# Moving one of four sums of squares from ScalarE to VectorE at the start of a hybrid encoder block

## The chip, the cores and the metric

The kernel runs on one NeuronCore of one Trainium2 chip. The metric is the time of one execution on the device in microseconds (us). Before the change the median of three runs is 943.38 us, the lowest 943.36 and the highest 943.39.

A core has five engines that run at the same time, each through its own list of instructions and strictly in the order of that list: TensorE (PE in the profile, with its weight loads as PEld), VectorE (DVE), ScalarE (ACT), GpSimd (POOL) and SyncE (SP), which here only issues transfers. An instruction that needs another engine's result waits for a semaphore, and everything behind it on its own engine waits with it.

## The reference

One layer is computed for 256 prompt tokens and 2048 sample tokens, each with 16 learned meta tokens in front. What matters here is its beginning: each token's row of 1024 numbers is divided by the root of the mean of its squares and weighted, and one large projection follows.

```python
def rmsnorm(x, w):
    xf = x.astype(jnp.float32)
    y = xf * lax.rsqrt(jnp.mean(xf * xf, axis=-1, keepdims=True) + NORM_EPS)
    return (y * w.astype(jnp.float32)).astype(x.dtype)

def hybrid_layer(z, norm_w, w_in, ...):
    h = rmsnorm(z, norm_w)
    proj = jnp.einsum('bld,de->ble', h, w_in)
    q, k, v, g_att, c_val, c_glu, g_conv = jnp.split(proj, SPLIT_IDX, axis=-1)
    ...  # windowed attention, gated convolution with layer norm, output projection
    return z + jnp.einsum('ble,ed->bld', mixed, w_out)
```

## The kernel before

The 2320 rows (16 meta tokens, then 18 blocks of 128 tokens) are worked in six groups of columns: the first has 400 (the meta tokens and blocks 1 to 3), the others 384. For each group the normalised rows are wanted transposed, split in a high and a low part (`xh`, `xl`), and then multiplied with eleven units of the input weights (`ws`, split in the same way; lines 863 and 879, tile `pj`). This projection, the attention and the output projection keep TensorE at work to the end.

The first group is made differently from the others, since nothing is there yet to hide it. For its four pieces `i` = 0 (16 meta rows) and 1 to 3 (128 rows each), which are called xn0 to xn3 here:

1. `stats(i)` issues the load of the rows (line 719) and returns a function `rest`. Called later, `rest` squares the rows on ScalarE and sums them along the row (`ssq`, line 726: an `ACTIVATE` and a short `ACTIVATION_READ_ACCUMULATOR`), and calls `rsqrt`, which is two GpSimd instructions: line 148 scales the sum and adds epsilon, line 149 raises it to the power of -1/2 and writes column `i` of `rstd`.
2. VectorE multiplies the rows with `rstd` (line 1131).
3. TensorE multiplies the identity a few times to stay busy (line 1096, `warmup`; 10, 5, 2 and 3 times, each in the trace two matmuls) and transposes the first six of the eight column blocks of 128 (line 1103, tile `xt`).
4. When all four pieces are transposed, ScalarE makes `xh` (line 1111) and VectorE `xl` (line 1113), block by block, between the same split of the first weights (lines 838 and 839), and TensorE starts on `pj`.

Pieces 4 to 6 (the second group) are squared later on ScalarE, at about 19 us; their `rstd` columns go through TensorE (line 755, tile `bc`) into the scaling of `xt` on VectorE (line 772).

The order on each engine is set by the tile framework's scheduler from its own estimate of the times, except for instructions that are "pinned" to program order (`pinned`, `keep_in_program_order`). The squares, the multiplications of line 1131 and the splits are pinned. The two instructions of `rsqrt` and most loads are not: where they stand on GpSimd and SyncE is the scheduler's decision at build time, and the chip keeps to it.

Tiles come from pools with a fixed number of buffers. `sp`'s tag `xn` has two; the loads of xn5 and xn6 took them in the kernel before.

Of the kernel before, what the change touches and what calls it, by code (L numbers as in the profile page):

```python
# [11 lines left out]
F32 = mybir.dt.float32  # L12
F32R = mybir.dt.float32r
BF16 = mybir.dt.bfloat16
AF = mybir.ActivationFunctionType
ALU = mybir.AluOpType
AX = mybir.AxisListType

P = 128
D = 1024  # L20
# [79 lines left out]
def hymba_kernel(  # L100
# [11 lines left out]
    nc = tc.nc  # L112
# [33 lines left out]
    def rsqrt(dst, src, scale, eps):  # L146
        n = src.shape[-1]
        nc.gpsimd.tensor_scalar(src, src, scale, eps, op0=ALU.mult, op1=ALU.add)  # L148
        nc.gpsimd.tensor_tensor(dst, src, half[: src.shape[0], 0:n], op=ALU.pow)
# [56 lines left out]
    sp = right_pools.enter_context(tc.tile_pool(name="sp", bufs=2, side="right"))  # L206
# [494 lines left out]
    if True:  # L701
# [3 lines left out]
        def pinned(op, yes=True):  # L705
            if yes:
                tc.keep_in_program_order(op)

        def stats(i):
            rows = NM if i == 0 else P  # L710
            r0 = 0 if i == 0 else NM + P * (i - 1)
            if i < 4:
                xn = cp.tile([P, UWID], F32, tag="us", name=f"xn{i}")[:, :D]
                rows0[i] = xn
            elif i == 4:
                xn = yp.tile([P, YW], F32, tag="y", name=f"xn{i}")[:, :D]
            else:
                xn = sp.tile([P, D], F32, tag="xn", name=f"xn{i}")
            dma = nc.sync.dma_start(xn[:rows], z[r0 : r0 + rows, :])
            if i >= PIN_X:  # L720
                tc.keep_in_program_order(dma)

            def rest():
                ssq = sp.tile([P, 1], F32, tag="ssq", name=f"ssq{i}", bufs=4)
                sq = sq0[:, :D] if i < 4 else xn
                pinned(nc.scalar.activation(sq[:rows], xn[:rows], AF.Square, accum_out=ssq[:rows]), i < 10)  # L726
                rsqrt(rstd[:rows, i : i + 1], ssq[:rows], 1.0 / D, EPS)

            return rest
# [363 lines left out]
        def busy(pt, n):  # L1093

            for _ in range(n):
                tc.keep_in_program_order(nc.tensor.matmul(pt[:, :P], ident, ident, start=True, stop=True))

        def turn0(i, d):

            o, rows = SEGS0[i]  # L1100
            if d not in cols0:
                cols0[d] = psum.tile([P, 512], F32, tag="cdcdabcd"[d], name=f"xt0_{d}")
            return nc.tensor.transpose(
                cols0[d][:, o : o + rows], rows0[i][:rows, P * d : P * d + P], ident[:rows, :rows]
            )
# [14 lines left out]
        r = {0: stats(0)}  # L1120
# [5 lines left out]
        nc.sync.dma_start(cw, conv_w)  # L1126
        warmup = psum.tile([P, 512], F32, tag="a", name="warmup")
        for i in range(4):
            r[i]()
            o, rows = SEGS0[i]  # L1130
            pinned(nc.vector.tensor_scalar(rows0[i][:rows], rows0[i][:rows], rstd[:rows, i : i + 1], None, op0=ALU.mult))
            busy(warmup, (10, 5, 2, 3)[i])
            for d in range(6):
                tc.keep_in_program_order(turn0(i, d))
        preps[0].alloc()
        r = {i: stats(i) for i in (4, 5, 6)}
# [56 lines left out]
        for i, (c, u, g) in enumerate(items):  # L1193
# [34 lines left out]
            if c == 0 and u in U_GA:  # L1228
                for k3 in range(3):
                    k = 10 + 3 * (3 * (u - U_GA[0]) + g) + k3  # L1230
# [84 lines left out]
```

## Time and profile before

| | us |
|---|---|
| median of the runs | 943.38 |
| the profiled execution | 943.95 |
| span of its instructions | 941.9 |
| TensorE busy in the span | 935.6 |
| VectorE busy | 744.4 |
| ScalarE busy | 421.8 |
| GpSimd busy | 293.3 |

The profiled execution took 0.57 us more than the median of the runs; 2.05 us of it lie outside the span of its instructions. The profile gives for every instruction the start in us from the span's beginning, the duration, the engine, the line of the kernel and the operation with its tiles; an idle time in front of an instruction stands behind it in brackets, with what ended it.

### The profile page before, as it was taken

The numbers are of one execution on the slowest core, as the hardware profiler recorded it, in microseconds if no ns is written. First come the engines' busy times: TensorE is split into PE (matmuls) and PEld (weight loads), VectorE is DVE, ScalarE is ACT, GpSimd is POOL, SyncE is SP. The second block draws the span as 40 slices with busy tenths as digits, with TensorE's granted clock in tenths as the row PEclk, the third lists the DMA queues.
The fourth block names the chain that finished last, engine by engine and source line by source line (L and its number), as shares of the span: only waits on it lengthen the run. The fifth ranks groups of instructions, "written<-read, shape, count | busy, mean of one in ns | idle before, by whom it ended". The sixth has DMA issues, their size and how long they took to land.

```text
span 941.9 us, 16665 instructions
## 1 busy us (share of the span) xinstructions
PE 935.6 (99%) x5794; PEld 886.3 (94%) x5794; DVE 744.4 (79%) x1263; ACT 421.8 (45%) x1160; POOL 293.3 (31%) x490
## 2 busy tenths in 40 slices
PE   9999999999999999999999999999999999999998
PEld 8999999999999999999999999988888888888887
DVE  5579999997977879999996655677777677767773
ACT  7432022253457751011111356666666666656661
POOL 4320000173558400000000553755433242333332
PEclk9999999999999999999999999999999999999999
DMA  8575345676656595233333697975666556655512
GB/s 306 170 253 217 134 176 176 217 269 251 182 185 189 182 312 182 90 113 134 140 128 123 159 327 225 395 240 159 200 188 172 151 165 196 188 159 148 163 62 68
DMA packets 146211, 176.49 MB, mean 187 GB/s; under 512 B 40816, under 2 KB 108736, under 8 KB 146000
## 3 DMA queue, kind: packets, MB, share of 16 engines
q1 hardware_dynamic: 146128, 175.43, 57.8%
q8 instruction: 46, 0.75, 0.3%
q14 instruction: 37, 0.30, 0.1%
HBM read 112.69 MB, written 62.70 MB: 186 GB/s over the span
## 4 chain that ended last, share of the span: by engine, by line
PE 94%; DMA 2%; DVE 1%; SPq 1%; issue 0%; ACT 0%; POOL 0%; DVEq 0%; ACTq 0%; POOLq 0%
PE pj L863 43%; PE y L609 21%; PE pj L879 13%; PE O L533 5%; PE S L383 4%; PE pT_c L499 2%; PE pT_m L499 2%; PE pT_x L499 1%; DMA cd<-zn 1%; DMA bias<-in_bias_c 1%; PE qT L383 1%; PE lnu L240 0%; DMA xn<-in_z 0%; PE lnt L221 0%; DVE xt L772 0%
## 5 line engine op out<-in xcount | busy, mean ns | idle before, releaser
L863 PE MATMUL pj<-xh,ws 128*128 128x384 f32 (+1 forms) x1536 | 395.9, 338 | 0.1
L946 DVE SCALAR_TENSOR_TENSOR y<-us,cw,y 128x1167 f32<-128x1167 f32 x240 | 329.0, 1427 | 0.4
L863 PEld LDWEIGHTS pj<-xh,ws 128*128 128x128 f32 x1536 | 280.0, 188 | 0.4 <-ACT xh L1111 0.4
L863 PE MATMUL pj<-xl,ws 128*128 128x384 f32 (+1 forms) x768 | 260.9, 340 | 0.1
L609 PE MATMUL y<-wo,rest 128*128 128x512 f32 (+1 forms) x672 | 172.7, 394 | 0.0
L879 PE MATMUL pj<-ws,xh 128*128 128x256 f32 (+1 forms) x880 | 164.2, 284 | 0.3 <-DVE kn L1037 0.3
L863 PEld LDWEIGHTS pj<-xl,ws 128*128 128x128 f32 x768 | 144.1, 188 | 0.5 <-DVE xl L801 0.4
L609 PEld LDWEIGHTS y<-wo,rest 128*128 128x128 f32 x672 | 117.5, 189 | 21.4 <-DVE rest L566 0.3
L879 PEld LDWEIGHTS pj<-ws,xh 128*128 128x128 f32 (+1 forms) x880 | 136.1, 187 | 1.1 <-issue 0.4
L879 PE MATMUL pj<-ws,xl 128*128 128x256 f32 (+1 forms) x440 | 124.3, 283 | 0.0
L441 DVE CUSTOM_DVE_ANT_0 sb<-S,bias,vec 128x304 f32<-128x304 f32 (+5 forms) x144 | 74.5, 517 | 33.8 <-PE S L383 31.5
L453 ACT ACTIVATE sb<-sb,nm 128x304 f32<-128x304 f32 (+5 forms) x144 | 77.8, 540 | 48.9 <-DVE nm L441 48.2
L971 ACT ACTIVATE go<-pj 128x384 f32<-128x384 f32 x48 | 23.5, 489 | 149.8 <-PE pj L863 142.3
L879 PEld LDWEIGHTS pj<-ws,xl 128*128 128x128 f32 (+1 forms) x440 | 82.2, 187 | 0.2
L479 POOL TENSOR_SCALAR sb<-sb,es 128x304 f32<-128x304 f32 (+5 forms) x144 | 73.1, 525 | 16.0 <-DVE es L466 13.1
L561 POOL TENSOR_TENSOR at<-at,ga 128x256 f32<-128x256 f32 x36 | 26.5, 737 | 164.0 <-DVE at L555 104.8
L148 POOL TENSOR_SCALAR ssk<-ssk 128x2 f32<-128x2 f32 x18 | 8.4, 465 | 210.0 <-ACT sqk L985 210.0
L383 PEld LDWEIGHTS S<-kw,q 128*128 128x128 f32 x288 | 53.2, 188 | 10.6
L383 PE MATMUL S<-kw,q 128*128 128x304 f32 (+5 forms) x288 | 62.8, 299 | 0.0
L148 POOL TENSOR_SCALAR ssq<-ssq 128x4 f32<-128x4 f32 (+2 forms) x55 | 23.5, 427 | 98.3 <-ACT xn L726 74.4
L906 ACT ACTIVATE sg<-pj 128x384 f32<-128x384 f32 (+1 forms) x24 | 11.8, 492 | 82.9 <-PE pj L863 82.0
L609 PE MATMUL y<-wo,mch 128*128 128x512 f32 x144 | 47.2, 409 | 0.0
(139 smaller groups left out, 1306.9 us busy)
## 6 DMA issues: line engine op xcount, KB each, us to landing
wd<-ws SPq DMA_DIRECT2D x36, 512.0 KB, 5.8
ws<-wd SPq DMA_DIRECT2D x36, 512.0 KB, 6.2
wraw<-in_w_in SPq DMA_DIRECT2D x52, 256.0 KB, 6.3
xn<-in_z SPq DMA_DIRECT2D x18, 512.0 KB, 5.5
gd<-go SPq DMA_DIRECT2D x48, 192.0 KB, 2.2
yo<-in_z SPq DMA_DIRECT2D x36, 256.0 KB, 3.9
out_y<-yo SPq DMA_DIRECT2D x35, 256.0 KB, 2.7
wo<-wod SPq DMA_DIRECT2D x16, 512.0 KB, 7.4
```

The lines of the kernel that those rows point to most:

```text
L148: nc.gpsimd.tensor_scalar(src, src, scale, eps, op0=ALU.mult, op1=ALU.add)
L383: r = f(*a, **k)
L441: nc.vector.tensor_tensor_reduce(out=sb[:, n, c0:c1], in0=ps[:, 0:w], in1=cst["bias"][:, kv, at + c0 : at + c1], scale=1.0, scalar=nsnk[:, ...
L453: nc.scalar.activation(sb[:, n, c0:c1], sb[:, n, c0:c1], AF.Exp, bias=nm[:, n : n + 1], scale=-1.0, accum_out=rs[:, n : n + 1],)
L479: nc.gpsimd.tensor_scalar(sb[:, k, a0:a1], sb[:, k, a0:a1], es[:, k : k + 1], 1.0, op0=ALU.mult, op1=ALU.mult)
L499: nc.tensor.transpose(pt[: c1 - c0, n, :], sbt[b, kv][:, n, c0:c1], ident)
L533: nc.tensor.matmul(opj[b, kv][:, n0:n1], t[:r, kv, :], p[:r, n0:n1], start=(k == "c" and i == 0), stop=(k == "x" and i == len(work) - 1),)
L561: nc.gpsimd.tensor_tensor(at[:, pr, :], at[:, pr, :], gat[b][:, pr, :], op=ALU.mult)
L609: nc.tensor.matmul(ps, mh[mi][:, e % 4, :], wo[e, wi][:, cols], start=(e == 4 and k == 0), stop=(e == 3 and k == 2),)
L863: nc.tensor.matmul(ps[:, :n], ws[:, d, wi, P * half_i : P * half_i + P], x[xi][:, d, o : o + n], start=(k == 0), stop=(k == 3 * ND - 1),)
L879: nc.tensor.matmul(ps[:rows, :UW], x[xi][:, d, o : o + rows], ws[:, d, wi, :], start=(k == 0), stop=(k == 3 * ND - 1),)
L946: nc.vector.scalar_tensor_tensor(y[:, yo + o0 : yo + o1], u[:, o0 + k : o1 + k], cw[:, j, k : k + 1], y[:, yo + o0 : yo + o1], op0=ALU.mul ...
```

## The change

For piece 2 the squares and their sum are made by one VectorE instruction pair instead (`tensor_tensor_reduce`: multiply the rows with themselves, add along the row). Its product is written to a buffer `sq2` of the pool tag `xn`. In program order piece 2's `rest` now comes right after piece 1's, ahead of piece 1's multiplication.

```diff
             def rest():
                 ssq = sp.tile([P, 1], F32, tag="ssq", name=f"ssq{i}", bufs=4)
                 sq = sq0[:, :D] if i < 4 else xn
-                pinned(nc.scalar.activation(sq[:rows], xn[:rows], AF.Square, accum_out=ssq[:rows]), i < 10)
+                if i == 2:
+                    sq2 = sp.tile([P, D], F32, tag="xn", name="sq2")
+                    op = nc.vector.tensor_tensor_reduce(
+                        out=sq2[:, :D], in0=xn, in1=xn, scale=1.0, scalar=0.0, op0=ALU.mult, op1=ALU.add, accum_out=ssq
+                    )
+                else:
+                    op = nc.scalar.activation(sq[:rows], xn[:rows], AF.Square, accum_out=ssq[:rows])
+                pinned(op, i < 10)
                 rsqrt(rstd[:rows, i : i + 1], ssq[:rows], 1.0 / D, EPS)
...
         for i in range(4):
-            r[i]()
+            for k in ((0,), (1, 2), (), (3,))[i]:
+                r[k]()
             o, rows = SEGS0[i]
             pinned(nc.vector.tensor_scalar(rows0[i][:rows], rows0[i][:rows], rstd[:rows, i : i + 1], None, op0=ALU.mult))
             busy(warmup, (10, 5, 2, 3)[i])
```

TensorE's list is the same as before, word for word. ScalarE's lacks one instruction pair. In three lists something moved. Names carry the piece's number and a running number behind the underscore; lines behind the edit are 7 or 8 higher in the kernel after.

GpSimd, the six instructions that make the three large pieces' `rstd`, before:

```order
L148 TENSOR_SCALAR ssq1_165<-ssq1_165 128x1
L149 TENSOR_TENSOR rstd_86<-ssq1_165,half_82 128x1
L148 TENSOR_SCALAR ssq2_181<-ssq2_181 128x1
L149 TENSOR_TENSOR rstd_86<-ssq2_181,half_82 128x1
L148 TENSOR_SCALAR ssq3_194<-ssq3_194 128x1
L149 TENSOR_TENSOR rstd_86<-ssq3_194,half_82 128x1
```

The same place after:

```order
L148 TENSOR_SCALAR ssq1_165<-ssq1_165 128x1
L149 TENSOR_TENSOR rstd_86<-ssq1_165,half_82 128x1
L148 TENSOR_SCALAR ssq3_195<-ssq3_195 128x1
L149 TENSOR_TENSOR rstd_86<-ssq3_195,half_82 128x1
L148 TENSOR_SCALAR ssq2_169<-ssq2_169 128x1
L149 TENSOR_TENSOR rstd_86<-ssq2_169,half_82 128x1
```

The scheduler put piece 3's pair ahead of piece 2's.

VectorE, from piece 0's multiplication to the first weights' low part, before:

```order
L1131 TENSOR_SCALAR xn0_111<-xn0_111,rstd_86 16x1024
L1131 TENSOR_SCALAR xn1_114<-xn1_114,rstd_86 128x1024
L1131 TENSOR_SCALAR xn2_116<-xn2_116,rstd_86 128x1024
L1131 TENSOR_SCALAR xn3_118<-xn3_118,rstd_86 128x1024
L839 TENSOR_TENSOR ws0_0_120<-wraw0_0_121,ws0_0_120 128x2x256
```

The same place after (`ISA` is the new pair: the products with their sum, and the read of the sum):

```order
L1139 TENSOR_SCALAR xn0_111<-xn0_111,rstd_86 16x1024
L728 ISA sq2_170,ssq2_169<-xn2_116 128x1024
L728 ISA ssq2_169 128x1
L1139 TENSOR_SCALAR xn1_114<-xn1_114,rstd_86 128x1024
L1139 TENSOR_SCALAR xn2_116<-xn2_116,rstd_86 128x1024
L1139 TENSOR_SCALAR xn3_118<-xn3_118,rstd_86 128x1024
L846 TENSOR_TENSOR ws0_0_120<-wraw0_0_121,ws0_0_120 128x2x256
```

The new pair stands ahead of piece 1's multiplication; the multiplications still run in the order 1, 2, 3.

SyncE, the loads of the second group's rows (`xn`) and columns (`xt1`), before:

```order
L719 DMA xn4_210<-in_z 128x1024
L719 DMA xn5_212<-in_z 128x1024
L719 DMA xn6_214<-in_z 128x1024
L743 DMA xt1_0_216<-in_zt 128x2x384
L743 DMA xt1_1_218<-in_zt 128x2x384
L743 DMA xt1_2_220<-in_zt 128x2x384
L743 DMA xt1_3_222<-in_zt 128x2x384
```

The same place after:

```order
L719 DMA xn4_211<-in_z 128x1024
L750 DMA xt1_0_217<-in_zt 128x2x384
L719 DMA xn5_213<-in_z 128x1024
L750 DMA xt1_1_219<-in_zt 128x2x384
L750 DMA xt1_2_221<-in_zt 128x2x384
L750 DMA xt1_3_223<-in_zt 128x2x384
L719 DMA xn6_215<-in_z 128x1024
```

`sq2` has one of the two `xn` buffers first, so the load of xn6 waits for VectorE's new pair and now comes last of the seven.

## The prediction

> **What bounds the kernel now.** I read the page's first part, then the busy time by stretches.
>
> ```profile
> span 941.9 us, 16665 instructions
> PE 935.6 (99%) x5794; PEld 886.3 (94%) x5794; DVE 744.4 (79%) x1263; ACT 421.8 (45%) x1160; POOL 293.3 (31%) x490
> 12.20:15.40 3.20, 3.16 (x18) 2.51 (x19) 3.20 (x6) 3.20 (x7) 0.34 (x4) 1.00 1.06 407
> 15.40:28.00 12.60, 12.60 (x72) 12.54 (x71) 7.37 (x12) 9.17 (x17) 5.63 (x9) 1.00 0.79 281
> 28.00:920.00 892.00, 890.93 (x5536) 845.90 (x5535) 722.94 (x1225) 398.79 (x1118) 278.08 (x457) 1.00 0.58 187
> ```
>
> The columns of a stretch are its length, then the busy time of PE, PEld, DVE, ACT and POOL. From 15.4 us on TensorE is never without work for long: 12.60 of 12.60 us, then 890.93 of 892.00, so 1.07 us idle in all. What starts this stream later ends the kernel later, up to those 1.07 us. The change sits ahead of it, so the timeline of the first 15 us decides, engine by engine. ScalarE first:
>
> ```profile
> 5.33 1.06 ACT L726 ACTIVATE sq<-xn 128x1024 f32<-128x1024 f32 x1 [1.38 <-DMA xn<-in_z]
> 6.60 1.06 ACT L726 ACTIVATE sq<-xn 128x1024 f32<-128x1024 f32 x1
> 7.90 1.06 ACT L726 ACTIVATE sq<-xn 128x1024 f32<-128x1024 f32 x1
> 11.55 1.08 ACT L1111 ACTIVATE xh<-xt,vec 128x400 fp32r<-128x400 f32 x2 [1.16 <-PE xt L1103]
> ```
>
> Then SyncE's queue, one of its rows and its waits (us in all, times, longest):
>
> ```profile
> 7.83 0.33 SPq L829 DMA_DIRECT2D wraw<-in_w_in  x1
> SPq L829 <- DMA xn<-in_z: 1.5, 2, 0.9
> ```
>
> The squares start 1.27 and 1.30 us apart, which looks like an engine that is full. It isn't: the queue's eighth weight load, issued at 7.83, had waited for an xn load, and the last square starts at 7.90, 0.07 later. So piece 3 lands at about 7.8 and releases its square itself; the square before it (6.60 + 1.06) was done by then. Then the way from the squares to TensorE, on GpSimd,
>
> ```profile
> 6.57 0.19 POOL L148 TENSOR_SCALAR ssq<-ssq 128x1 f32<-128x1 f32 x1 [1.71 <-ACT sq L726]
> 6.84 0.57 POOL L149 TENSOR_TENSOR rstd<-ssq,half 128x1 f32<-128x1 f32 x1
> 7.84 0.41 POOL L148 TENSOR_SCALAR ssq<-ssq 128x1 f32<-128x1 f32 x1 [0.43 <-ACT sq L726]
> 8.33 0.56 POOL L149 TENSOR_TENSOR rstd<-ssq,half 128x1 f32<-128x1 f32 x1
> 9.13 0.59 POOL L148 TENSOR_SCALAR ssq<-ssq 128x1 f32<-128x1 f32 x1 [0.25 <-ACT sq L726]
> 9.80 0.54 POOL L149 TENSOR_TENSOR rstd<-ssq,half 128x1 f32<-128x1 f32 x1
> ```
>
> on VectorE,
>
> ```profile
> 7.44 0.75 DVE L1131 TENSOR_SCALAR xn<-xn,rstd 128x1024 f32<-128x1024 f32 x1 [1.81 <-POOL rstd L149]
> 8.92 0.75 DVE L1131 TENSOR_SCALAR xn<-xn,rstd 128x1024 f32<-128x1024 f32 x1 [0.72 <-POOL rstd L149]
> 10.38 0.75 DVE L1131 TENSOR_SCALAR xn<-xn,rstd 128x1024 f32<-128x1024 f32 x1 [0.71 <-ACT ws L838]
> ```
>
> and on TensorE:
>
> ```profile
> 8.25 0.88 PE L1103 MATMUL xt<-ident,xn 128*128 128x128 f32 x6 [0.36 <-DVE xn L1131]
> 9.73 0.87 PE L1103 MATMUL xt<-ident,xn 128*128 128x128 f32 x6 [0.15 <-DVE xn L1131]
> 10.44 0.83 PE L1096 MATMUL warmup<-ident 128*128 128x128 f32 x6
> 11.19 0.88 PE L1103 MATMUL xt<-ident,xn 128*128 128x128 f32 x6
> ```
>
> Piece 2 goes sum (7.84), `rstd` done (8.89), multiplied (8.92), transposed (9.73); piece 3 goes 9.13, 10.34, 10.38, 11.19, then `xh` at 11.55. The last multiplication's bracket names ACT's `ws`, but `rstd` was done at 10.34, right ahead of it, as with the two pieces before. Each piece is worked while the next one lands.
>
> **What the change costs, part by part.**
>
> *Taken from ScalarE:* one square with its read, 1.27 us. It brings nothing: piece 3's square can't start before its landing, and stays at 7.90, with its sum on GpSimd at 9.13 as now. Behind it ScalarE waits for TensorE's transposes anyway (1.16 us ahead of `xh`).
>
> *Added on VectorE:* a product-and-sum of 1024 columns from SBUF. The nearest rows are the same instruction from PSUM at 176 to 336 columns and the convolution's two-input step:
>
> ```profile
> L441 DVE CUSTOM_DVE_ANT_0 sb<-S,bias,vec x144: 386/526/570, 579.8 to 914.3; 128x304 f32<-128x304 f32 x84, 128x336 f32<-128x336 f32 x28, 128x176 f32<-128x176 f32 x8, 128x208 f32<-128x208 f32 x8
> L946 DVE SCALAR_TENSOR_TENSOR y<-us,cw,y 128x1167 f32<-128x1167 f32 x240 | 329.0, 1427 | 0.4
> ```
>
> From 386 ns at 176 to 570 at 336 it is 1.15 ns a column, which gives 570 + 688 x 1.15 = 1.36 us; L946 in proportion gives 1427 x 1024/1167 = 1.25 us. I keep both ends. It starts when piece 2 has landed, about 6.55, and ends at 7.80 to 7.91. Piece 1's multiplication stands behind it: ready at 7.44, it starts about 0.4 us late or more. That alone costs nothing, since piece 2's transposes, next on TensorE, come much later (below).
>
> *Moved on GpSimd, and this decides:* piece 3's pair now stands ahead of piece 2's. Piece 2's sum is ready at about 7.9, but GpSimd waits for ScalarE's sum of piece 3 until 9.13 with piece 2's pair queued behind; VectorE's multiplication of piece 2 waits for that, the one of piece 3 behind it, and TensorE for both. How long two pairs take one behind the other is seen with the second group:
>
> ```profile
> 22.51 0.19 POOL L148 TENSOR_SCALAR ssq<-ssq 128x1 f32<-128x1 f32 x1
> 23.42 0.19 POOL L148 TENSOR_SCALAR ssq<-ssq 128x1 f32<-128x1 f32 x1
> L1103 PE MATMUL xt<-ident,xn x32: 207/273/329, 5.9 to 15.1; 128*128 128x128 f32 x24, 16*128 16x16 f32 x8
> ```
>
> From start to start 0.91 us. So: piece 3's pair at 9.13; piece 2's at 10.04; its `rstd` done at 10.04 + 0.27 + 0.57 = 10.88; multiplied from 10.91; its transposes 0.81 later as now (8.92 to 9.73), at 11.72. Then six transposes (0.71, from 9.73 to 10.44) and six warmups of 0.11 (0.67) end at 13.10. Piece 3's rows, multiplied right behind piece 2's, are ready by 10.91 + 0.67 + 0.75 = 12.33, so its transposes start at 13.10 unhindered: 1.91 us later than 11.19. A transpose that didn't wait takes 0.27 instead of 0.33 us, so `xh` starts 0.05 less late: 1.86.
>
> *The port.* In the rows above line 148 takes 0.19 us, but 0.41 and 0.59 while VectorE multiplies: 7.84 + 0.41 = 8.25 is 0.06 after VectorE's end at 8.19, 9.13 + 0.59 = 9.72 is 0.05 after 9.67. With two inputs from SBUF, as the new instruction has:
>
> ```profile
> 185.05 8.16 DVE L946 SCALAR_TENSOR_TENSOR y<-us,cw,y 128x1167 f32<-128x1167 f32 x6
> 185.85 7.40 POOL L148 TENSOR_SCALAR ssq<-ssq 128x1 f32<-128x1 f32 x1 [65.16 <-ACT xn L726]
> ```
>
> a 0.19 us instruction took 7.40. Piece 1's sum comes to GpSimd at 6.57 and the new instruction to VectorE at about 6.55. If VectorE is first, that sum ends 0.05 after 7.80 to 7.91, `rstd` 0.65 later, and piece 1's multiplication runs from 8.53 to 9.28, or from 8.64 to 9.39. It then covers 9.13, when piece 3's sum starts, which ends at 9.33 to 9.44 instead of 9.32: 0.01 to 0.12 us more. [...]
>
> *Moved on SyncE:* xn6 comes behind four loads of 384 KB, in the place of the last `xt` load.
>
> ```profile
> 12.48 2.38 SPq L743 DMA_DIRECT2D xt<-in_zt  x4
> xt<-in_zt SPq DMA_DIRECT2D x4, 384.0 KB, 8.9
> 21.11 1.09 ACT L726 ACTIVATE xn<-xn 128x1024 f32<-128x1024 f32 x1
> 23.69 0.54 POOL L149 TENSOR_TENSOR rstd<-ssq,half 128x1 f32<-128x1 f32 x1
> 27.17 0.49 PE L755 MATMUL bc<-ident,rstd 128*128 128x128 f32 x3
> ```
>
> Issued at about 14.9 with 8.9 us to landing, it lands near 23.8; its square, at 21.11 now and 23.0 after the shift, may wait 0.8. Its `rstd` is then ready at 24.23 + 1.9 + 0.8 = 26.9, and TensorE wants it at 27.17 + 1.9 = 29.1. The cover is 2.1 us; I cost it at nothing. Behind that square on ScalarE stands the first sigmoid (line 906); on TensorE's list the next user of the bank it reads comes after `bc`. Behind xn6 on SyncE stands xn7's load, which waits for a square on ScalarE in either order. If the cover were gone, `bc` would be late next, microsecond for microsecond.
>
> *Sum.* From `xh` on everything hangs on ScalarE's and TensorE's own lists (12.2 to 15.4: ScalarE 3.20 of 3.20 busy) and shifts as a whole. I take 1.86 + 0.07 for the port = 1.93 us. The profiled execution, 943.95 us with a span of 941.9, would take 945.88; it lies 0.57 above the median of 943.38, so the median becomes 945.3. Its own range, 1.86 to 1.98 with some 0.1 for landings that vary, is 945.1 to 945.5.
>
> 0.2%, about what a measurement of this kernel can tell from no change, is 1.89 us: 945.27. The forecast lies almost on it.
>
> **Rivals.**
>
> *The shift is taken in later (not slower).* TensorE's 1.07 us of idle time between 28 and 920 stands for the most part in two waits:
>
> ```profile
> PE lnu L240 <- DVE zn L234: 0.7, 1, 0.7
> PE pj L879 <- DVE kn L1037: 0.3, 1, 0.3
> ```
>
> If their releasers don't shift, all of it goes: 945.31 - 1.07 = 944.24. It decides from 0.04 us on (1.93 against 1.89). Against it: both releasers work on results that TensorE made, which shift too. I give it 0.08.
>
> *ScalarE was the bound after all.* If piece 3 has landed by 6.6, its square starts at 6.60, its pair at 7.84 and piece 2's `rstd` is done at 7.84 + 0.41 + 0.08 + 0.56 + 0.91 = 9.80 instead of 10.88: the shift is 0.8 us, 944.2. The queue's row at 7.83 speaks against it. I give it 0.03.
>
> *TensorE's clock falls back.* At the start it ran at half speed:
>
> ```profile
> 1.36 4.63 PE L1096 MATMUL warmup<-ident 128*128 128x128 f32 x20 [1.36 <-POOL ident masks.py:199]
> 6.51 1.38 PE L1096 MATMUL warmup<-ident 128*128 128x128 f32 x10
> ```
>
> 4.63 us for 20, then 1.38 for 10, of which some 0.2 is the wait and the last one's end: 0.23 and 0.11 to 0.14 each. In the changed kernel TensorE stands still for 1 to 2 us before 11.72. If that costs it the full clock for as long as at the start (4.63 us), 2.3 us are lost, or half of that where ScalarE sets the pace anyway: 946.5 to 947.6. The pause of 0.36 us ahead of 8.25 kept the clock; no row here shows a longer one. [...] I give it 0.06.
>
> **Numbers.** The main case has 0.80, of which 0.48 above 945.27 and 0.32 below; taken in later 0.08, ScalarE the bound 0.03, clock 0.06; 0.03 stay for a gain that I see no row for (at most the 0.40 us that line 148 loses at 9.13, 943.0, or a cause not seen). Slower 0.54, the same 0.43, faster 0.03. The range 944.2 to 946.0 takes in the main case and the first two rivals.
>
> **What would show it.** After: the square of piece 3 still at 7.90; GpSimd's sums in the order 1, 3, 2, with piece 2's at 10.0 to 10.2; VectorE idle until 10.9 and then two multiplications in a row; the third `xt` group at 11.7, the fourth at 13.1, `xh` at 13.4 to 13.5; line 148 for piece 1 over 1 us long if VectorE was first. Wrong would be a piece 2 pair that ends before 9.13, `pj` running at 0.36 us a matmul at 14 us, or idle times of TensorE behind 28 us that differ from 1.07.

## The result and the profile after

Against the kernel before on the same chip the changed kernel took 947.14 us in the median of five executions (944.82 to 947.95), the one before 943.38: a ratio of 1.0035, 95% interval 1.002 to 1.005. It is slower, and by more than forecast (945.3, range 944.2 to 946.0). Two later comparisons gave 1.002 (1.0010 to 1.0029; 945.48 us, inside the forecast range, against 944.18) and 1.0028 (1.0018 to 1.0037; 946.55 against 943.91 us). Of the twelve executions of one version below, with both pauses filled, two were in a slow state (1316 and 1878 us), and its figures leave them out.

The profiled execution took 945.87 us, close to the sum forecast for it (945.88). The page and the busy time by stretches, with the columns as before:

```profile
span 943.8 us, 16664 instructions
```

```profile
12.20:15.40 3.20, 3.03 (x24) 2.42 (x22) 2.09 (x5) 1.94 (x4) 0.00 (x0) 1.00 1.05 398
15.40:28.00 12.60, 12.60 (x72) 12.31 (x72) 8.99 (x14) 10.70 (x20) 5.99 (x12) 1.00 0.78 265
28.00:920.00 892.00, 891.06 (x5538) 846.18 (x5537) 722.07 (x1223) 399.90 (x1118) 279.30 (x455) 1.00 0.59 187
```

The span is 1.9 us longer. TensorE's idle time behind 28 us is nearly what it was (0.94 for 1.07), so the 1.9 us arise ahead of `pj`. The timeline of the first 15 us, rows of VectorE, GpSimd, ScalarE and TensorE by their start:

```profile
6.62 1.23 DVE L728 CUSTOM_DVE_ANT_0 sq<-xn 128x1024 f32<-128x1024 f32 x1 [0.94 <-DMA xn<-in_z]
6.63 1.26 POOL L148 TENSOR_SCALAR ssq<-ssq 128x1 f32<-128x1 f32 x1 [1.73 <-ACT sq L732]
...
7.96 1.06 ACT L732 ACTIVATE sq<-xn 128x1024 f32<-128x1024 f32 x1 [1.41 <-DMA xn<-in_z]
...
9.19 0.20 POOL L148 TENSOR_SCALAR ssq<-ssq 128x1 f32<-128x1 f32 x1 [0.64 <-ACT sq L732]
9.39 0.87 PE L1110 MATMUL xt<-ident,xn 128*128 128x128 f32 x6 [1.43 <-DVE xn L1139]
...
10.11 0.19 POOL L148 TENSOR_SCALAR ssq<-ssq 128x1 f32<-128x1 f32 x1
10.39 0.54 POOL L149 TENSOR_TENSOR rstd<-ssq,half 128x1 f32<-128x1 f32 x1
10.97 1.42 DVE L1139 TENSOR_SCALAR xn<-xn,rstd 128x1024 f32<-128x1024 f32 x2 [1.63 <-POOL rstd L149]
11.77 0.87 PE L1110 MATMUL xt<-ident,xn 128*128 128x128 f32 x6 [1.06 <-DVE xn L1139]
12.48 0.83 PE L1103 MATMUL warmup<-ident 128*128 128x128 f32 x6
13.15 0.82 PE L1110 MATMUL xt<-ident,xn 128*128 128x128 f32 x6
13.46 1.08 ACT L1118 ACTIVATE xh<-xt,vec 128x400 fp32r<-128x400 f32 x2 [3.28 <-PE xt L1110]
```

VectorE started the new instruction at 6.62; GpSimd's sum of piece 1, started at 6.63, took 1.26 us instead of 0.19 and ended 0.04 us behind it. Piece 3's square waits for its landing as before (7.96). GpSimd then takes piece 3's sum (9.19) and only after it piece 2's (10.11), which VectorE waited for, idle for 1.63 us, and TensorE behind it. `xh` starts at 13.46 instead of 11.55. ScalarE's missing square left only a longer wait ahead of `xh`: 3.28 us for 1.16.

That explains 945.87, not a median of 947.14. In three of the first five executions the mean granted clock of TensorE was 0.996 to 0.998 and the times 947.14 to 947.95; the other two had 1.00, 944.82 and 945.87. Over the 26 executions of the changed kernel in this study the 10 with 1.00 have a median of 945.57 us, the 16 below it 946.64. (A single stretch of 3.41 us at half speed brings the mean to 0.998. Two of the 16 stand at 0.999, which 7 of 96 executions of the kernel before beside these runs show as well; the other 14 are at 0.998 or 0.996.)

### The profile page after: what moved, and what is told of

The parts are those of the page before. It is cut to its first block, busy times and chain, and to the rows that moved or that the text cites. A ratio compares the mean times of both kernels' runs of the same rounds, so it can differ in the third digit from the quotient of the medians.

```text
span 943.8 us, 16664 instructions
## 1 busy us (share of the span) xinstructions
PE 935.7 (99%) x5794; PEld 886.3 (94%) x5794; DVE 745.5 (79%) x1265; ACT 421.7 (45%) x1158; POOL 295.7 (31%) x490
## 4 chain that ended last, share of the span: by engine, by line
PE 93%; DMA 3%; SPq 1%; DVE 1%; issue 1%; ACT 0%; POOL 0%; DVEq 0%; ACTq 0%; POOLq 0%
PE pj L870 43%; PE y L609 21%; PE pj L886 13%; PE O L533 5%; PE S L383 4%; PE pT_c L499 2%; PE pT_m L499 2%; PE pT_x L499 1%; DMA cd<-zn 1%; DMA bias<-in_bias_c 1%; PE qT L383 1%; DMA xn<-in_z 1%; PE lnu L240 0%; PE lnt L221 0%; DVE xt L779 0%
## 5 line engine op out<-in xcount | busy, mean ns | idle before, releaser
L479 POOL TENSOR_SCALAR sb<-sb,es 128x304 f32<-128x304 f32 (+5 forms) x144 | 73.5, 529 | 15.9 <-DVE es L466 13.1
```

Source lines behind the costliest of these rows:

```text
L479: nc.gpsimd.tensor_scalar(sb[:, k, a0:a1], sb[:, k, a0:a1], es[:, k : k + 1], 1.0, op0=ALU.mult, op1=ALU.mult)
```

## The experiments

**Which part of the change makes `xh` late.** The changed kernel with the first instruction of piece 3's pair pinned behind piece 2's, so that GpSimd goes 1, 2, 3 again:

```diff
-    def rsqrt(dst, src, scale, eps):
+    def rsqrt(dst, src, scale, eps, keep=False):
         n = src.shape[-1]
-        nc.gpsimd.tensor_scalar(src, src, scale, eps, op0=ALU.mult, op1=ALU.add)
+        op = nc.gpsimd.tensor_scalar(src, src, scale, eps, op0=ALU.mult, op1=ALU.add)
+        if keep:
+            tc.keep_in_program_order(op)
...
-                rsqrt(rstd[:rows, i : i + 1], ssq[:rows], 1.0 / D, EPS)
+                rsqrt(rstd[:rows, i : i + 1], ssq[:rows], 1.0 / D, EPS, i == 3)
```

> The changed kernel with GpSimd's pairs pinned in the order of pieces 1, 2, 3; VectorE still makes piece 2's sum. Theory A (GpSimd's order costs most, and the port blocking of line 148 the rest): piece 1's sum still ends only with VectorE's new instruction at 7.9, piece 2's pair is held by VectorE's multiplication of piece 1 until 9.4, piece 3's by that of piece 2 until 10.85, so the fourth transposes start at about 12.3 instead of 13.15, and the kernel takes 944.5 us where it keeps the clock. Rival (order alone, no port blocking): fourth transposes at 10.9, 943.0 to 943.2 us. Rival (VectorE's instruction itself is the cost, the order nothing): 945.3 or more, as the changed kernel.

944.83 us, ratio 1.0016 (1.0008 to 1.0025). Its timeline on GpSimd and VectorE, and the first `xh`:

```profile
6.65 1.27 POOL L148 TENSOR_SCALAR ssq<-ssq 128x1 f32<-128x1 f32 x1 [1.77 <-ACT sq L734]
8.61 0.75 DVE L1141 TENSOR_SCALAR xn<-xn,rstd 128x1024 f32<-128x1024 f32 x1 [0.73 <-POOL rstd L151]
8.66 0.75 POOL L148 TENSOR_SCALAR ssq<-ssq 128x1 f32<-128x1 f32 x1
...
10.08 0.75 DVE L1141 TENSOR_SCALAR xn<-xn,rstd 128x1024 f32<-128x1024 f32 x1 [0.72 <-POOL rstd L151]
...
10.13 0.75 POOL L148 TENSOR_SCALAR ssq<-ssq 128x1 f32<-128x1 f32 x1
...
12.72 1.08 ACT L1120 ACTIVATE xh<-xt,vec 128x400 fp32r<-128x400 f32 x2 [1.90 <-PE xt L1112]
```

With the order put right `xh` is still 1.17 us late (12.72 against 11.55): piece 1's sum takes 1.27 us for 0.19 beside the new instruction, and each later sum starts 0.05 us after a multiplication on VectorE and ends 0.05 us behind its end (0.75 us for 0.19). So the order alone isn't the whole: with it put right, the new instruction on VectorE still delays `xh`. What the order does by itself is the next run.

The kernel before, all squares on ScalarE, with piece 3's pair pinned ahead of piece 2's (`rsqrt` takes `keep` as above, here for piece 2):

```diff
-                rsqrt(rstd[:rows, i : i + 1], ssq[:rows], 1.0 / D, EPS)
+                late = lambda: rsqrt(rstd[:rows, i : i + 1], ssq[:rows], 1.0 / D, EPS, i == 2)
+                if i == 2:
+                    return late
+                late()
...
-            r[i]()
+            if i < 2:
+                r[i]()
+            elif i == 2:
+                late = r[2]()
+                r[3]()
+                late()
```

> The kernel before, all four squares on ScalarE, with GpSimd's pairs pinned in the order of pieces 1, 3, 2. Theory A (the order is what shifts the start): piece 2's rstd is ready at 10.9 as in the changed kernel, fourth transposes at 13.0 to 13.15, 945.2 us where the clock is kept; TensorE has one pause of about 2.1 us from 9.6 to 11.7, so some runs lose the clock and take 946.5 to 948. Rival (VectorE's instruction and the port are the cost): 943.4 us.

946.23 us, ratio 1.0023 (1.0013 to 1.0033). Its timeline, and the stretch behind it:

```profile
9.17 0.19 POOL L148 TENSOR_SCALAR ssq<-ssq 128x1 f32<-128x1 f32 x1 [1.71 <-ACT sq L728]
10.93 1.42 DVE L1141 TENSOR_SCALAR xn<-xn,rstd 128x1024 f32<-128x1024 f32 x2 [2.69 <-POOL rstd L151]
11.74 1.20 PE L1108 MATMUL xt<-ident,xn 128*128 128x128 f32 x6 [2.12 <-DVE xn L1141]
12.73 1.49 PE L1101 MATMUL warmup<-ident 128*128 128x128 f32 x6
14.01 1.49 PE L1108 MATMUL xt<-ident,xn 128*128 128x128 f32 x6
```

```profile
12.20:15.60 3.40, 3.40 (x17) 3.38 (x16) 1.25 (x3) 1.13 (x3) 0.00 (x0) 0.51 1.05 406
```

Without any work moved to VectorE the order gives the multiplications at 10.93 and the third transposes at 11.74: the changed kernel's 10.97 and 11.77. Each of the two faults would by itself make TensorE's start late, the order by more (third transposes at 11.74, against 10.89 in the run before this one and 9.73 in the kernel before). And here the clock fell to half from 12.14 to 15.56: the same six warmups and six transposes take 1.49 us each instead of 0.83, and `xh` came 1.0 us later than in the changed kernel (14.47).

**Does a pause of 1 to 2 us cost the clock by itself?** The kernel before without the warmups behind pieces 0 and 1, its GpSimd order as it was:

```diff
-            busy(warmup, (10, 5, 2, 3)[i])
+            busy(warmup, (10, 0, 0, 3)[i])
```

> The kernel before without the warmups in front of piece 1's and piece 2's transposes (10, 0, 0, 3 instead of 10, 5, 2, 3), so that TensorE pauses about 1.6 us before 8.25 and 0.6 us before 9.73 while nothing it waits for moves. Theory A (pauses lose the clock, independent of any shift): some of the runs with a mean granted clock below 1 and 1 to 4 us over 943.4, the others 943.4. Rival (pauses of this length cost nothing): all runs 943.0 to 943.6 with clock 1.000.

945.27 us, ratio 1.0016 (1.0007 to 1.0024); nine of eleven executions below 1.00; the two at 1.00 took longest, 946.24 and 946.32 us. The profiled one:

```profile
8.33 1.14 PE L1103 MATMUL xt<-ident,xn 128*128 128x128 f32 x6 [1.98 <-DVE xn L1131]
```

```profile
8.80:12.20 3.40, 3.07 (x15) 2.67 (x14) 2.11 (x3) 0.94 (x3) 1.29 (x3) 0.50 1.03 387
```

A pause of 1.98 us, with half speed from 8.79 to 12.21 behind it, was enough, with nothing else changed. The opposite, the changed kernel with both pauses filled by warmups:

```diff
-            busy(warmup, (10, 5, 2, 3)[i])
+            busy(warmup, (10, 11, 6, 3)[i])
```

> The changed kernel with more warmups in front of piece 1's and piece 2's transposes (11 and 6 instead of 5 and 2), so that TensorE has next to no pause of 1.43 and 1.06 us there; all else the same. Theory A (the runs of 947 to 948 us lost TensorE's full clock in those pauses): granted clock 1.000 in every run, all runs within about 0.4 us of each other, 945.2 to 945.9. Theory B (the excess over 945.3 has another cause, such as the later load of xn6): the runs still spread up to 947 or 948 with a mean clock below 1.

945.58 us, ratio 1.002 (1.0011 to 1.0029), the clock at 0.999 or 1.00 in all. But the times ranged from 944.74 to 946.75 and not within the 0.4 us expected, and the profiled execution took 946.01 with `xh` at 14.81:

```profile
6.67 4.68 PE L1103 MATMUL warmup<-ident 128*128 128x128 f32 x22
11.19 0.82 PE L1110 MATMUL xt<-ident,xn 128*128 128x128 f32 x6
```

22 warmups took 4.68 us, 0.21 each: the clock's first rise, at 6.2 and 6.4 us in the profiles of before and after, came at 10.81 here, and the mean granted clock counts from that rise on, so it reads 1.00. TensorE's own warmups then made the transposes late. Each pause filled alone, and the first one emptied:

```diff
-            busy(warmup, (10, 5, 2, 3)[i])
+            busy(warmup, (10, 11, 2, 3)[i])   # first run
+            busy(warmup, (10, 5, 6, 3)[i])    # second run
+            busy(warmup, (10, 0, 2, 3)[i])    # third run
```

> The changed kernel with eleven warmups instead of five behind piece 1's transposes, which fill the pause of 1.43 us; that of 1.06 us stays. No window of 3.41 us can then be busy less than 0.65. Theory of the busy share: the clock is kept in every execution, 944.7 to 945.9 us. Rival (a pause of 1 us is enough by itself): some executions at 0.998 and above 946.5.

> The changed kernel with six warmups instead of two behind piece 2's transposes' place on TensorE's list, which fill the pause of 1.06 us or most of it; that of 1.43 us stays. No window of 3.41 us can then be busy less than 0.54. Theory of the busy share, with a threshold somewhere between 0.41 (fell) and 0.58 (kept): clock kept in all or nearly all executions, 944.7 to 945.9 us; if some fall, the threshold is above 0.54. Rival (the longest pause decides, and 1.43 us is too long): about as many executions at 0.998 as in the changed kernel.

> The changed kernel with no warmups behind piece 1's transposes instead of five: the first pause grows by about 1.1 us to some 2.5 us, idle 3.6 us in all between 6.9 and 11.8. Wherever the windows of 3.41 us fall, one of them is busy at most 0.47. Theory of the busy share: nearly every execution loses the clock for one or two windows, 946 to 948 us, median above that of the changed kernel. Rival (a pause must last a full window of 3.41 us): no execution loses it, 944.8 to 945.9 us.

> The changed kernel once more, unedited, beside the three below. Its two pauses of TensorE (1.43 us ending at 9.39, 1.06 us ending at 11.77) lie within 3.81 us, so a window of 3.41 us can hold up to 2.1 us of them, a busy share of 0.38, or as little as 1.06. Theory of the busy share (a window of 3.41 us, counted from the first rise of the clock, that was busy well under a half is followed by one at half speed): where the windows fall differs from execution to execution, so some show a granted clock of 1.00 and 944.8 to 945.9 us, the others 0.998 and 946.5 to 948. Rival (the earlier spread came from that chip's state): all executions alike, within 0.3 us.

The first three are the edits above, the fourth is the changed kernel unedited. First filled: 945.96 us, every execution at 1.00 (944.55 to 946.66; the upper ones above what was expected), so the pause of 1.05 us that it keeps lost the clock in none. Second filled: 945.35 us, two of eleven below 1.00 (0.999 and 0.998). First emptied: 946.89 us, four of six at 0.996 or 0.998, the two at 1.00 no shorter (946.60 and 947.33). The changed kernel beside them: 945.48 us, four of nine below 1.00, one of these at 0.996 and 948.15 us, the other three only 945.11 to 945.42. So the clock follows the pauses. But a lower mean doesn't say what it costs, and keeping it did not bring the medians clearly below the changed kernel's. To see that, four more profiles of the changed kernel were taken:

> The changed kernel, unedited, for one profile more: of its first five executions three took 947.1 to 948.0 us and no profile shows such a one. Theory (clock): the time is the start of pj on TensorE plus about 925.3 us of work plus idle time behind it plus a tail of 3.2 us; a granted clock of 1.00 gives xh at 13.4 to 13.6 and 944.8 to 945.9 us; a half-speed window that ends before 13 gives about 14.0, one that lies between 12 and 16 about 14.5, two of them more, and with up to 1.1 us of idle time later 946 to 947.5. Rival (something behind 30 us): xh as in the profile after, and idle time or work behind it that is 1 to 2 us longer.

> As look_a: each execution has its own phase of the windows. Clock theory: its xh is late by what the half-speed windows took, and the rest of the time is alike within the 1 us of TensorE's later idle time. Rival: the rest differs by 1 to 2 us.

> As look_a and look_b, a third execution with its own phase of the windows.

> As look_a and look_b, a fourth execution with its own phase of the windows.

The table splits the profiled executions of this kernel, e5 and a later one, e12, among them: start of `xh`, TensorE's work and its idle time from the first `pj` to its last matmul; from there to the end of the span it is 3.16 or 3.17 us in each.

| | clock at half speed | `xh` | work | idle | us |
|---|---|---|---|---|---|
| look_a | until 10.36 | 13.42 | 925.60 | 0.92 | 945.77 |
| first profile | until 6.41 | 13.46 | 925.55 | 0.97 | 945.87 |
| look_d | until 6.07, 9.48 to 12.89 | 13.97 | 925.18 | 0.42 | 945.40 |
| e5 | until 6.03, 9.45 to 12.86 | 14.03 | 925.15 | 0.40 | 945.42 |
| look_c | until 4.22, 11.05 to 14.46 | 14.72 | 925.22 | 0.66 | 946.42 |
| e12 | until 4.54, 11.36 to 14.78 | 14.73 | 925.30 | 0.63 | 946.49 |
| look_b | until 5.51, 8.93 to 15.75 | 14.85 | 925.20 | 0.73 | 946.66 |

The clock explains `xh`: a half-speed stretch over by 12.9 costs 0.5 to 0.6 us, one that covers the third and fourth transposes 1.3 to 1.4. In work and idle time together these executions have 0.6 to 1.0 us less than the first profile, so look_d and e5, clock lost, ended ahead of it. TensorE's wait that varies most, in the first profile after (us in all, times, longest):

```profile
PE lnu L240 <- DVE zn L234: 0.6, 1, 0.6
```

This wait of the first profile was 0.66 us in the kernel before, 1.0 in the run with few warmups, and missing in look_d (in the run with few warmups the profile names ScalarE as what ended it). look_b on TensorE:

```profile
9.40 1.54 PE L1110 MATMUL xt<-ident,xn 128*128 128x128 f32 x6 [1.80 <-DVE xn L1139]
10.74 1.06 PE L1103 MATMUL warmup<-ident 128*128 128x128 f32 x4
11.78 1.54 PE L1110 MATMUL xt<-ident,xn 128*128 128x128 f32 x6
13.11 1.49 PE L1103 MATMUL warmup<-ident 128*128 128x128 f32 x6
14.39 1.49 PE L1110 MATMUL xt<-ident,xn 128*128 128x128 f32 x6
```

**What decides on the clock.** In all these profiles it changes only at multiples of 3.41 us from its first rise. Sorted by TensorE's busy share, the windows of 3.41 us that lost the clock (0.32 to 0.61) overlap with those that kept it (from 0.53). Counted in matmuls of 128 columns, each where it starts (piece 0's transposes have 16 columns and count an eighth), they don't: from full speed, windows with 3.75, 5.75, 10, 11.5, 11.6 and 11.75 lost it, those with 13, 13.75, 14.1 and more kept it; from half speed, 12 and less stayed there, and the rise came from 13 on (13 itself went both ways). The late rise of e1 fits: its window from 3.98 to 7.39 was busy throughout, but six of its matmuls had 16 columns, and it counts 11.75. This rule was read off the runs, all of them with fp32 matmuls in these windows, so it was tried on new ones:

```diff
-            busy(warmup, (10, 5, 2, 3)[i])
+            busy(warmup, (10, 7, 4, 3)[i])    # first run
+            busy(warmup, (10, 5, 2, 3)[i])    # second run: as before, and
+            for _ in range((0, 10, 8, 0)[i]):
+                tc.keep_in_program_order(nc.tensor.matmul(warmup[:, :4], ident, ident[:, :4], start=True, stop=True))
```

> The changed kernel with seven warmups instead of five and four instead of two behind pieces 1's and 2's place, that is four matmuls of 128 columns more in each pause. The pauses shrink from 1.43 and 1.06 us to about 1.0 and 0.6, both in 3.4 us. Theory of the columns (a window of 3.41 us keeps the clock if at least 12 to 13 matmuls of 128 columns stream through the array in it): every window has 13.5 or more, the clock is kept in every execution (1.00), 944.7 to 945.9 us. Theory of the busy share: windows with both pauses are busy 0.53, below the 0.55 to 0.61 at which the clock was lost in e5 and look_b, so some executions at 0.998 or less.

> The changed kernel with ten and eight more warmups behind pieces 1's and 2's, each of only 4 columns instead of 128 (in the trace two matmuls each, at about 0.06 us), so that the pauses of 1.43 and 1.06 us are nearly full of work that streams almost nothing: 36 x 4 columns are 1.1 matmuls of 128. Theory of the columns: windows still have 10 to 12.5, the clock is lost in about as many executions as in the changed kernel (10 of 18 so far show less than 1.00). Theory of the busy share: TensorE is busy 0.9 in every window, the clock is kept in every execution.

> The changed kernel, unedited, on the chip of e10 and e11, so that the share of executions with less than the full clock is seen beside theirs. Both theories: about half of them, 945.1 to 945.9 us with the full clock and up to 948 without.

Four warmups more in each pause: all seven executions at 1.00, as the columns have it; the changed kernel beside them had it at 0.998 in five of eight and at 0.999 in one (946.55 us). But the seven still ranged from 944.53 to 948.50 us (median 946.31), against the 944.7 to 945.9 expected, so a mean clock of 1.00 did not by itself make them short. The first rise isn't mended by these warmups: in the profiled execution it came at 10.38, behind a window from 3.55 to 6.97 that counts 11.75, as in e1. Yet that execution is the one of 944.53 us, the shortest, so the late rise isn't shown to be what made the others long. The narrow fill: 951.70 us, four of six executions at 0.994 to 0.996, and the other two longer still, at 1.00. The profile of one of these, 955.41 us:

```profile
8.97 4.27 PE L1142 MATMUL warmup<-ident 128*128 128x4 f32 x20
13.10 1.52 PE L1110 MATMUL xt<-ident,xn 128*128 128x128 f32 x6
15.26 3.41 PE L1142 MATMUL warmup<-ident 128*128 128x4 f32 x16
18.54 1.52 PE L1110 MATMUL xt<-ident,xn 128*128 128x128 f32 x6
```

```profile
6.00:24.60 18.60, 18.60 (x88) 18.04 (x89) 6.38 (x11) 5.26 (x12) 3.32 (x6) 1.00 0.86 312
```

TensorE was busy for 18.60 of 18.60 us and stayed at half speed up to 24.61 (six transposes in 1.52 us; the 1.00 in the row stands there because no change is recorded ahead of the first rise). Here being busy did not raise the clock; the rise came at the end of the window from 21.20 to 24.61, the first to count well over 13 (20.6). The times were missed: a matmul of 4 columns took 0.21 us, as long as one of 128, not 0.06, so the fill made TensorE itself late.

**The shift without the clock.** Both kernels with piece 0's narrow transposes moved behind piece 1's warmups, and in the changed one three warmups more in each pause, so that every window that lies wholly behind TensorE's first warmup should count 13 or more:

```diff
-            busy(warmup, (10, 5, 2, 3)[i])
-            for d in range(6):
-                tc.keep_in_program_order(turn0(i, d))
+            busy(warmup, (10, 5, 2, 3)[i])    # in the changed kernel (10, 8, 5, 3)
+            for k in ((), (0, 1), (2,), (3,))[i]:
+                for d in range(6):
+                    tc.keep_in_program_order(turn0(k, d))
```

> The kernel before with piece 0's six transposes (16 columns each) moved behind piece 1's warmups, so that TensorE begins with 30 warmups of 128 columns on end. Theory of the columns: the first whole window always reaches 13, the clock rises by 8.2 us at the latest and is kept; 943.0 to 944.0 us with less spread than before, whose late executions (above 944.4) are gone. Rival (the spread of before has nothing to do with the first rise): the same spread, 942.8 to 945.7.

> The changed kernel with the same move and with warmups (10, 8, 5, 3), so that each of its pauses has 0.66 us less. Theory of the columns: clock up by 8.4 us and kept in every execution, so that the difference to e13 is the shift on GpSimd alone, 1.6 to 2.0 us less what idle time at 575 us gives back (up to 0.7): 944.7 to 945.8 us, xh at 13.4 to 13.6, none above 946.2. Rival (something else makes executions of the changed kernel long): some at 946.5 to 948 as before.

Before so arranged: 943.33 us (942.76 to 944.12), ratio to before 1.000 (0.9991 to 1.0009). After so arranged: 945.38 us (944.93 to 946.46), ratio 1.002 (1.0011 to 1.0029), no execution below 0.999. The first `xh` of the one and of the other:

```profile
11.58 1.08 ACT L1111 ACTIVATE xh<-xt,vec 128x400 fp32r<-128x400 f32 x2 [1.28 <-PE xt L1103]
```

```profile
13.74 1.08 ACT L1118 ACTIVATE xh<-xt,vec 128x400 fp32r<-128x400 f32 x2 [3.10 <-PE xt L1110]
```

With the clock kept the difference of the medians is 2.05 us, and nothing reaches 947. Two expectations for the changed kernel were missed by a little: one execution lies above 946.2, and `xh` in the profile above 13.6, where piece 3's square began 0.32 us later than in the other profile (8.21 and 7.89), behind its landing. No version here beats the kernel before; e13 equals it, with a smaller spread in its eleven executions (before beside it: 942.83 to 945.17 in 21).

## Why the prediction was wrong

**The step that failed is the rival "TensorE's clock falls back", given 0.06.** A pause was forecast (still for 1 to 2 us before 11.72; measured 1.06), and the price nearly so (946.5 to 947.6; look_b and look_c took 946.66 and 946.42, the first median was 947.14). The other pause, 1.43 us ahead of piece 1's transposes, follows from the prediction's own times for piece 1 (multiplied until 9.28 or later), but there it "alone costs nothing". Every window in which the profiles of the changed kernel lost the clock holds all or most of this pause; with it filled all eleven executions kept 1.00, with the other one filled nine of eleven. Wrong was the ground for its chance. "The pause of 0.36 us ahead of 8.25 kept the clock; no row here shows a longer one" left the length open, and the low chance was the author's estimate alone. In the runs the clock moves in steps of 3.41 us whose place differs from execution to execution (behind the first rise, half speed began at 8.93, 9.45, 9.48, 11.05 and 11.36 us in the profiles of the changed kernel), and a pause of 1.5 to 1.8 us lost it there, with the window 39% to 61% busy and never empty. In 14 of 26 executions the mean clock is 0.998 or less. With that chance the likeliest case would have been a mixture reaching to 948, and the range had to go there. How many executions of a comparison lose the clock, and how much, is chance: one of the later medians, 945.48 us, lies inside the range.

**The main term held.** Points, forecast and measured in the first profile: piece 3's square 7.90 and 7.96; piece 2's pair 10.0 to 10.2 and 10.11; third `xt` group 11.7 and 11.77, fourth 13.1 and 13.15; `xh` later by 1.86 to 1.98, and 1.91; the execution 945.88 and 945.87. The last agreement is partly luck: 0.06 of the 1.91 us came from piece 3's later landing, which the sum didn't have, and the sum's 0.07 for the port was 0.01 (piece 3's sum took 0.20 us for 0.19). With the clock kept in both kernels it is 2.05 us between medians.

**The port** is the author's name for a cause that no run shows; the runs show line 148 ending 0.04 to 0.06 us behind the VectorE instruction it started beside. The delay was sized rightly: VectorE was first (6.62, GpSimd 6.63), and line 148 took 1.26 us. The new instruction took 1.23 us, a little under both bounds (1.25 and 1.36). What the prediction didn't say is that with the order unchanged the new instruction would still have made `xh` 1.17 us late (12.72 in e2): under the shift of the order nearly all of it is hidden.

**The moved load** cost nothing, as forecast. xn6's square waited 0.73 us for its landing (0.8 forecast), and TensorE's `bc` came at 27.17 + 1.90:

```profile
23.90 1.06 ACT L732 ACTIVATE xn<-xn 128x1024 f32<-128x1024 f32 x1 [0.73 <-DMA xn<-in_z]
29.07 0.49 PE L762 MATMUL bc<-ident,rstd 128*128 128x128 f32 x3
```

**Taken in later:** against it stood that both releasers shift too, and in the first profile 0.94 of 1.07 us remained. But the wait at `lnu` isn't a fixed amount (0 to 1.0 us between profiles, in kernels with and without the change). It widens every forecast by about half a microsecond to both sides. Landings vary too: in the seven profiles of the changed kernel piece 3's square began between 7.84 and 8.07. The prediction's "some 0.1 for landings that vary" was too little, and three executions of before, 0.03 us apart, hid a spread of 942.8 to 945.7.

**ScalarE the bound:** refuted; piece 3's square stayed at its landing.

Open: no execution above 947 was profiled. The largest profiled shift from the clock (1.4 us) with the longest `lnu` wait seen would reach about 947.3; the five executions of the changed kernel from 947.4 to 948.2, and one with four warmups more at 948.50 and 1.00, need more. A first rise even later than 10.8 us is a candidate for the five, not shown; that no execution reached 947 where every window counts 13 would fit it. For the 948.50 it explains little, since with those warmups the window behind piece 0's transposes counts 16 in the profile. The longer executions of the kernel before (up to 945.67 at 1.00) are unexplained in the same way.

## What to carry to other kernels

When a change makes TensorE wait ahead of its main stream, cost the clock along with the wait (here `xh` came up to 1.4 us later by it): count the columns of the matmuls that start in any window of 3.41 us that may fall there (from full speed, windows with at most 11.75 times 128 lost the clock here, those with 13 or more kept it), and take the worst placing of the window, since here the place differed from execution to execution. The count of 13 was seen in this kernel's fp32 warmups and transposes alone. Look at the scheduler's order on the small engine between two big ones: one swapped pair on GpSimd cost 1.9 us, where the square taken from ScalarE gave nothing because a landing released the last one. And a time on which a verdict of 0.2% hangs needs more than three executions on either side.

## What was not expected of the hardware

- From full speed, half speed followed windows of 3.41 us in which at most 11.75 matmuls of 128 columns started, with TensorE 32% to 61% busy, and none with 13 or more; in e11 it lasted to 24.61 us with TensorE 100% busy from 6 us on, 36 of its matmuls having 4 columns.
- The mean granted clock leaves out the time ahead of the first rise: the profiles had the first rise at 4.2 to 10.8 us, e1 at 10.81 with a mean of 1.00, and e11 at 24.61, also with 1.00.
- At half speed a matmul of 4 columns took as long as one of 128: 0.21 us.
- GpSimd's 0.19 us instruction that started 0.05 us behind a one-input multiplication of VectorE took 0.75 us, twice (e2): it ended 0.05 us behind that instruction, as beside the two-input one (1.27 us, 0.04 behind).
